# Fused waits, a later release of held stores, and two chunks taken whole, in a row-normalisation kernel on one core

One Trainium2 (trn2) chip, one core. The metric is the device time of the kernel in microseconds (us), of the slowest core, which here is the only one. "Span" is the profiled execution from first to last instruction; it is some 1.3 us shorter than the time.

## The reference

```python
# x: 16 x 1024 x 512 float32, gamma: 512 ones, eps: 1e-5
rms = np.sqrt(np.mean(x ** 2, axis=-1, keepdims=True) + eps)
return np.maximum(x / rms * gamma, 0)
```

That is 33.55 MB in and 33.55 MB out, and a few operations per element.

## The kernel before

The 16,384 rows are cut into 8 chunks; a chunk gives each of the 128 partitions 16 rows (32 KB), 4.19 MB in all. The kernel keeps room for six chunks ("slots") in SBUF. SyncE issues all loads and stores into one DMA queue. GpSimd passes "loaded" on to ScalarE, which squares and sums 8 rows at a time (a group) and takes the root. VectorE takes the reciprocal, scales 8 rows by 8 instructions, clamps the group at zero by a ninth (the relu), and reports `done`. Two waits hold stores back (groups, chunks and stores are counted from 0): stores 0 and 1 until the third row of group 5 (`tick3`), store 2 and all later ones until the first row of group 10 (`tick1`). Loads 6 and 7 reuse the slots of stores 0 and 1.

```python
def take(engine, sem, n):              # one separate semaphore instruction
    engine.wait_ge(sem, n)
    engine.sem_inc(sem, -n)
...
nc.sync.wait_ge(tick3, 6)
store(0)
store(1)
for s in range(2):
    nc.sync.wait_ge(sem_slot[s], 32)
    load(7 + s)                        # loads of chunks 6 and 7
nc.sync.wait_ge(tick1, 11)
for i in range(2, nchunks):
    store(i)                           # each waits for its chunk's two groups
...
with nc.vector.Fori(0, ngroups) as gi: # 16 groups
    take(nc.vector, sq, 1)
    ...
    nc.vector.reciprocal(out=rstd[...], in_=rms[...]).then_inc(sv, 1)
    take(nc.vector, sv, 1)
    for j in range(G):                 # 8 rows of 512
        r = nc.vector.scalar_tensor_tensor(out=row, in0=row, scalar=rstd[...],
                in1=gamma_sb, op0=ALU.mult, op1=ALU.mult)
        ...                            # j == 0: tick1, j == 2: tick3, j == 7: sv
    take(nc.vector, sv, 1)
    nc.vector.tensor_scalar_max(out=blk, in0=blk, scalar1=0.0).then_inc(done, 1)
```

Of the kernel before, what the change touches and what calls it, by code (L numbers as in the profile page):

```python
# [1 line left out]

# [4 lines left out]

F32 = mybir.dt.float32
ALU = mybir.AluOpType
ACTF = mybir.ActivationFunctionType  # L10


@with_exitstack
def kernel(
    ctx: ExitStack,
    tc: tile.TileContext,
    x: bass.AP,
    gamma: bass.AP,
    eps: bass.AP,
    out: bass.AP,  # L20
):




    nc = tc.nc
    P = nc.NUM_PARTITIONS

    x2 = x.flatten_outer_dims()
    out2 = out.flatten_outer_dims()  # L30
    n, d = x2.shape
    rows = n // P
    inv_d = 1.0 / d
    K = 16
    G = 8
    nchunks = rows // K
    nslots = 6
    ngroups = rows // G
    per = K // G
    xv = x2.rearrange("(c p k) d -> c p k d", p=P, k=K)  # L40
    ov = out2.rearrange("(c p k) d -> c p k d", p=P, k=K)

    def sbuf(name, shape):
        return nc.alloc_sbuf_tensor(name, shape, F32).ap()

    gseed = sbuf("gseed", [P, d])
    gamma_sb = sbuf("gamma_sb", [P, d])
    eps_sb = sbuf("eps_sb", [P, 1])
    ss = sbuf("ss", [P, rows])
    rms = sbuf("rms", [P, rows])  # L50
    rstd = sbuf("rstd", [P, rows])
    slots = sbuf("slots", [P, nslots * K * d])
    junk = nc.alloc_psum_tensor("junk", [P, G, d], F32).ap()


    loads = [(0, 0, G), (0, G, K - G)] + [(i, 0, K) for i in range(1, nchunks)]


    sem_half = nc.alloc_semaphore("half")
    sem_slot = [nc.alloc_semaphore(f"slot{s}") for s in range(nslots)]  # L60
    sem_g = nc.alloc_semaphore("gam")
    sem_z = nc.alloc_semaphore("zero")
    ready = nc.alloc_semaphore("ready")
    sq = nc.alloc_semaphore("sq")
    tick1 = nc.alloc_semaphore("tick1")
    tick3 = nc.alloc_semaphore("tick3")
    done = nc.alloc_semaphore("done")
    sa = nc.alloc_semaphore("sa")
    sv = nc.alloc_semaphore("sv")

    def slot_ap(i):
        s = (i % nslots) * K * d
        return slots[:, s:s + K * d].rearrange("p (k d) -> p k d", d=d)

    def load(m):
        i, a, r = loads[m]
        return nc.sync.dma_start(out=slot_ap(i)[:, a:a + r, :],
                                 in_=xv[i][:, a:a + r, :]
                                 ).then_inc(sem_half if m == 0 else sem_slot[i % nslots], 16)

    def take(engine, sem, n):
        engine.wait_ge(sem, n)
        engine.sem_inc(sem, -n)  # L83

    def store(i):
        nc.sync.wait_ge(done, per * (i + 1))
        nc.sync.dma_start(out=ov[i], in_=slot_ap(i)).then_inc(sem_slot[i % nslots], 16)



    ctx.enter_context(tc.manual_schedule(engines={mybir.EngineType.SP}))
    early = 2
    for m in range(early):
        t = load(m)
        tc.no_tile_sem_insts.add(t.ins.name)
    ctx.close()
    tc.close()
    tc.compile()  # L98

    for m, (i, a, r) in enumerate(loads):  # L100
        if m >= early and i < nslots:
            load(m)


    nc.sync.wait_ge(tick3, 6)
    store(0)
    store(1)
    for s in range(2):
        nc.sync.wait_ge(sem_slot[s], 32)
        load(7 + s)  # L110
    nc.sync.wait_ge(tick1, 11)
    for i in range(2, nchunks):
        store(i)

    for m, (i, a, r) in enumerate(loads):
        if m == 0:
            take(nc.gpsimd, sem_half, 16)
        else:
            nc.gpsimd.wait_ge(sem_slot[i % nslots], 32 * (i // nslots) + 16)
        nc.gpsimd.sem_inc(ready, r // G)  # L120

    nc.vector.memset(gseed, 0.0).then_inc(sem_z, 1)  # L122
    nc.vector.memset(eps_sb, eps).then_inc(sem_z, 1)  # L123

    nc.scalar.wait_ge(sem_z, 1)
    nc.scalar.dma_start(out=gseed[0:P:32, :],
                        in_=gamma[None, :].to_broadcast([P // 32, d])
                        ).then_inc(sem_g, 16)
    nc.scalar.preload_act_table(ACTF.Sqrt)  # L129
    take(nc.scalar, sem_z, 2)  # L130
    with nc.scalar.Fori(0, ngroups) as gi:
        take(nc.scalar, ready, 1)
        base = nc.scalar.snap((gi % (nslots * per)) * (G * d))
        col = nc.scalar.snap(gi * G)
        for j in range(G):
            a = nc.scalar.activation(  # L136
                out=junk[:, j, :], in_=slots[:, bass.ds(base + j * d, d)],
                func=ACTF.Square, accum_out=ss[:, bass.ds(col + j, 1)])
            if j == G - 1:
                a.then_inc(sa, 1)  # L140
        take(nc.scalar, sa, 1)
        nc.scalar.activation(out=rms[:, bass.ds(col, G)], in_=ss[:, bass.ds(col, G)],  # L142
                             func=ACTF.Sqrt, bias=eps_sb, scale=inv_d).then_inc(sq, 1)

    take(nc.vector, sem_g, 16)
    nc.vector.stream_shuffle(gamma_sb, gseed, [0] * 32)  # L146
    with nc.vector.Fori(0, ngroups) as gi:
        take(nc.vector, sq, 1)
        base = nc.vector.snap((gi % (nslots * per)) * (G * d))
        col = nc.vector.snap(gi * G)  # L150
        blk = slots[:, bass.ds(base, G * d)]
        nc.vector.reciprocal(out=rstd[:, bass.ds(col, G)],  # L152
                             in_=rms[:, bass.ds(col, G)]).then_inc(sv, 1)
        take(nc.vector, sv, 1)
        for j in range(G):
            row = slots[:, bass.ds(base + j * d, d)]
            r = nc.vector.scalar_tensor_tensor(  # L157
                out=row, in0=row, scalar=rstd[:, bass.ds(col + j, 1)], in1=gamma_sb,
                op0=ALU.mult, op1=ALU.mult)
            if j == 0:  # L160
                r.then_inc(tick1, 1)
            if j == 2:
                r.then_inc(tick3, 1)
            if j == G - 1:
                r.then_inc(sv, 1)
        take(nc.vector, sv, 1)
        nc.vector.tensor_scalar_max(out=blk, in0=blk, scalar1=0.0).then_inc(done, 1)  # L167

    take(nc.sync, done, ngroups)
    take(nc.sync, tick1, ngroups)  # L170
    take(nc.sync, tick3, ngroups)
    for i in range(nchunks - nslots, nchunks):
        take(nc.sync, sem_slot[i % nslots], 32 * (i // nslots + 1))


# [1 line left out]
_INS = ['x', 'gamma', 'eps']  # L177
_OUTS = [((16, 1024, 512), 'float32')]

_NUMBERS = {'eps': 9.999999747378752e-06}  # L180


# [26 lines left out]
```

## Time and profile before

| | before |
|---|---|
| time, median of 4 runs (lowest to highest) | 160.50 us (160.39 to 160.58) |
| span | 159.3 us |
| VectorE busy, share | 126.0 us, 79% |
| ScalarE busy, share | 86.3 us, 54% |
| share of the 16 DMA engines taken by the queue of loads and stores | 98.2% |
| mean rate of loads and stores together | 421 GB/s |

The share of the DMA engines is 98.2%, while VectorE, the busiest engine, has a fifth of the span idle. Beside the profile's pages I use two records that the trace holds: each DMA packet (start, length, size; 2,176 of them are data) and each instruction, the sequencers' own among them. "First packet" below is the first data packet of a load or a store; the queue "runs dry" when it has nothing left to move. To know how busy an engine was I lay the packets end to end on 16 engines, as the trace does not name the engine.

### The profile page before, as it was taken

The page shows a single profiled execution, that of the slowest core. Times are in us where ns is not written, and L with a number is a line of the kernel's source. Part 1 is how long each engine was busy: PE and PEld are TensorE (multiplying, and loading weights), DVE is VectorE, ACT ScalarE, POOL GpSimd, SP SyncE. Part 2 cuts the span into 40 slices and gives each one's busy share as a digit, 9 for nine tenths or more (in the row PEclk, how much of TensorE's full clock was granted, in tenths as well). Part 3 has the DMA queues.
Part 4 walks back from the last instruction along what each step waited for, and adds up shares of the span by engine and source line. Part 5 has one row for each costly group of instructions (what it writes and reads, how often), then busy time and mean ns, then how long its engine had stood idle before and what let it go on. Part 6 is the DMA issues. An engine that isn't in the chain of part 4 may idle for free. (4 is left out here: it accounts for less than half of the span.)

```text
span 159.3 us, 999 instructions
## 1 busy us (share of the span) xinstructions
DVE 126.0 (79%) x164; ACT 86.3 (54%) x273; POOL 0.2 (0%) x4
## 2 busy tenths in 40 slices
DVE  1012989898999999999999999999999989897000
ACT  0388929889989988988920098898500000000000
POOL 0000000000000000000000000000000000000000
DMA  6999999999999999999999999999999999999995
GB/s 193 405 453 424 502 395 395 502 420 395 453 469 395 395 502 420 395 428 494 395 395 444 461 411 395 486 436 395 453 453 403 411 494 411 403 461 453 395 420 247
DMA packets 2456, 67.12 MB, mean 421 GB/s; under 512 B 276, under 2 KB 276, under 8 KB 280
## 3 DMA queue, kind: packets, MB, share of 16 engines
q1 hardware_dynamic: 2448, 67.11, 98.2%
q10 hardware_dynamic: 8, 0.01, 0.0%
HBM read 33.56 MB, written 33.55 MB: 421 GB/s over the span
## 5 line engine op out<-in xcount | busy, mean ns | idle before, releaser
L157 DVE SCALAR_TENSOR_TENSOR slots<-slots,rstd,gamma_sb 128x512 f32 x128 | 86.2, 747 | 4.8 <-DVEq L83 4.8
L136 ACT ACTIVATE junk<-slots 128x512 f32 x128 | 74.4, 581 | 20.6 <-ACTq L83 20.3
L167 DVE TENSOR_SCALAR slots<-slots x16 | 36.7, 2294 | 2.4 <-DVEq L83 0.2
L136 ACT ACTIVATION_READ_ACCUMULATOR junk<-slots x128 | 23.9, 187 | 0.0
L152 DVE RECIPROCAL rstd<-rms x16 | 3.1, 197 | 5.3 <-DVEq L83 5.3
L142 ACT ACTIVATE rms<-ss,eps_sb x16 | 4.8, 301 | 3.0 <-ACTq L83 3.0
L146 DVE LOAD_MASK_SELECT gamma_sb<-gseed x1 | 0.0, 14 | 5.4 <-DVEq L83 5.4
L129 ACT ACT_TABLE_LOAD x1 | 1.3, 1283 | 4.2 <-issue 4.2
L122 DVE MEMSET gseed<- 128x512 f32 x1 | 0.5, 485 | 2.6 <-PEq L98 2.6
L146 DVE STREAM_SHUFFLE gamma_sb<-gseed 128x512 f32<-128x512 f32 x1 | 0.7, 723 | 0.0
L190 POOL MEMSET const-bfloat16-1.0<- 128x1 bf16 x1 | 0.1, 102 | 0.0
L190 POOL MEMSET const-uint8-127<- 128x1 uint8 x1 | 0.1, 102 | 0.0
L190 POOL MEMSET const-float32-0.0<- 128x1 f32 x1 | 0.1, 99 | 0.2 <-issue 0.2
L190 POOL MEMSET const-float32-1.0<- 128x1 f32 x1 | 0.1, 99 | 0.0
L123 DVE MEMSET eps_sb<- 128x1 f32 x1 | 0.1, 59 | 0.0
## 6 DMA issues: line engine op xcount, KB each, us to landing
out_dram<-slots SPq DMA_DIRECT2D x8, 4096.0 KB, 20.6
slots<-in_x_dram SPq DMA_DIRECT2D x7, 4096.0 KB, 29.7
slots<-in_x_dram SPq DMA_DIRECT2D x2, 2048.0 KB, 9.7
gseed<-in_gamma_dram ACTq DMA_DIRECT2D x1, 8.0 KB
```

The costliest lines, as they stand in the source:

```text
L122: nc.vector.memset(gseed, 0.0).then_inc(sem_z, 1)
L123: nc.vector.memset(eps_sb, eps).then_inc(sem_z, 1)
L129: nc.scalar.preload_act_table(ACTF.Sqrt)
L136: a = nc.scalar.activation(out=junk[:, j, :], in_=slots[:, bass.ds(base + j * d, d)], func=ACTF.Square, accum_out=ss[:, bass.ds(col + j, 1)])
L142: nc.scalar.activation(out=rms[:, bass.ds(col, G)], in_=ss[:, bass.ds(col, G)], func=ACTF.Sqrt, bias=eps_sb, scale=inv_d).then_inc(sq, 1)
L146: nc.vector.stream_shuffle(gamma_sb, gseed, [0] * 32)
L152: nc.vector.reciprocal(out=rstd[:, bass.ds(col, G)], in_=rms[:, bass.ds(col, G)]).then_inc(sv, 1)
L157: r = nc.vector.scalar_tensor_tensor(out=row, in0=row, scalar=rstd[:, bass.ds(col + j, 1)], in1=gamma_sb, op0=ALU.mult, op1=ALU.mult)
L167: nc.vector.tensor_scalar_max(out=blk, in0=blk, scalar1=0.0).then_inc(done, 1)
L190: nc = _bacc.Bacc("TRN2", target_bir_lowering=False, num_devices=1)
```

## The change

Its intent is to spend less of VectorE's time on waiting and on starting instructions. Waits no longer go by a separate instruction, but stand in front of the instruction that is to carry them, with the decrements moved to the end of the group. One tick at the sixth row (`G - 3`) replaces the two at the third and the first. The last two chunks are taken whole, by a reciprocal, a multiplication and a custom multiply-and-clamp. Two memsets move from VectorE to GpSimd. As the loop now ends before a slot is used again, its slot index no longer needs a remainder (`gi % 12` becomes `gi`). Cut to its core:

```diff
-    nc.sync.wait_ge(tick3, 6)
+    nc.sync.wait_ge(tick, 6)
...
-    nc.sync.wait_ge(tick1, 11)
+    nc.sync.wait_ge(tick, 11)
...
-    with nc.vector.Fori(0, ngroups) as gi:
-        take(nc.vector, sq, 1)
+    with nc.vector.Fori(0, ndyn) as gi:          # ndyn = 12
+        nc.vector.wait_ge(sq, 1)
         nc.vector.reciprocal(...).then_inc(sv, 1)
-        take(nc.vector, sv, 1)
+        nc.vector.wait_ge(sv, 1)
         for j in range(G):
             ...
-            if j == 0:
-                r.then_inc(tick1, 1)
-            if j == 2:
-                r.then_inc(tick3, 1)
-            if j == G - 1:
-                r.then_inc(sv, 1)
-        take(nc.vector, sv, 1)
+            if j == G - 3:
+                r.then_inc(tick, 1)
+        r.then_inc(sv, 1)
+        nc.vector.wait_ge(sv, 2)
         nc.vector.tensor_scalar_max(out=blk, in0=blk, scalar1=0.0).then_inc(done, 1)
+        nc.vector.sem_inc(sv, -2)
+        nc.vector.sem_inc(sq, -1)
+    for i in range(nslots, nchunks):             # chunks 6 and 7
+        nc.vector.wait_ge(sq, per * (i - nslots + 1))
+        nc.vector.reciprocal(out=fac, in_=rms[:, i * K:(i + 1) * K]).then_inc(sv, 1)
+        nc.vector.wait_ge(sv, steps + 1)
+        nc.vector.tensor_tensor(out=blk, in0=blk, in1=fac[...to P, K, d], op=ALU.mult).then_inc(sv, 1)
+        nc.vector.wait_ge(sv, steps + 2)
+        nc.vector._custom_dve(dve_ops.TENSOR_MUL_SAT, out=blk, in0=blk,
+            in1=gamma_sb[...to P, K, d], s0=float("inf"), s1=0.0).then_inc(done, per)
```

(ScalarE's loop gets the same treatment of its waits.)

More of the change, by code (lines that the diff above doesn't have):

```diff
@@ L4 @@
 import concourse.tile as tile
-from concourse import bass_utils, mybir
+from concourse import bass_utils, dve_ops, mybir
 from concourse._compat import with_exitstack
@@ L64 @@
     sq = nc.alloc_semaphore("sq")
-    tick1 = nc.alloc_semaphore("tick1")
-    tick3 = nc.alloc_semaphore("tick3")
+    tick = nc.alloc_semaphore("tick")
     done = nc.alloc_semaphore("done")
@@ L110 @@
         load(7 + s)
-    nc.sync.wait_ge(tick1, 11)
+    nc.sync.wait_ge(tick, 11)
     for i in range(2, nchunks):
         store(i)
+    nc.gpsimd.memset(gseed, 0.0).then_inc(sem_z, 1)
+    nc.gpsimd.memset(eps_sb, eps).then_inc(sem_z, 1)
     for m, (i, a, r) in enumerate(loads):
@@ L120 @@
         nc.gpsimd.sem_inc(ready, r // G)
-    nc.vector.memset(gseed, 0.0).then_inc(sem_z, 1)
-    nc.vector.memset(eps_sb, eps).then_inc(sem_z, 1)
     nc.scalar.wait_ge(sem_z, 1)
@@ L131 @@
     with nc.scalar.Fori(0, ngroups) as gi:
-        take(nc.scalar, ready, 1)
         base = nc.scalar.snap((gi % (nslots * per)) * (G * d))
         col = nc.scalar.snap(gi * G)
+        nc.scalar.wait_ge(ready, 1)
         for j in range(G):
@@ L138 @@
                 func=ACTF.Square, accum_out=ss[:, bass.ds(col + j, 1)])
-            if j == G - 1:
-                a.then_inc(sa, 1)
-        take(nc.scalar, sa, 1)
+        a.then_inc(sa, 1)
+        nc.scalar.wait_ge(sa, 1)
         nc.scalar.activation(out=rms[:, bass.ds(col, G)], in_=ss[:, bass.ds(col, G)],
                              func=ACTF.Sqrt, bias=eps_sb, scale=inv_d).then_inc(sq, 1)
-    take(nc.vector, sem_g, 16)
+        nc.scalar.sem_inc(sa, -1)
+        nc.scalar.sem_inc(ready, -1)
+    nc.vector.wait_ge(sem_g, 16)
     nc.vector.stream_shuffle(gamma_sb, gseed, [0] * 32)
-    with nc.vector.Fori(0, ngroups) as gi:
-        take(nc.vector, sq, 1)
-        base = nc.vector.snap((gi % (nslots * per)) * (G * d))
+    ndyn = nslots * per
+    with nc.vector.Fori(0, ndyn) as gi:
+        base = nc.vector.snap(gi * (G * d))
         col = nc.vector.snap(gi * G)
         blk = slots[:, bass.ds(base, G * d)]
+        nc.vector.wait_ge(sq, 1)
         nc.vector.reciprocal(out=rstd[:, bass.ds(col, G)],
                              in_=rms[:, bass.ds(col, G)]).then_inc(sv, 1)
-        take(nc.vector, sv, 1)
+        nc.vector.wait_ge(sv, 1)
         for j in range(G):
@@ L159 @@
                 op0=ALU.mult, op1=ALU.mult)
-            if j == 0:
-                r.then_inc(tick1, 1)
-            if j == 2:
-                r.then_inc(tick3, 1)
-            if j == G - 1:
-                r.then_inc(sv, 1)
-        take(nc.vector, sv, 1)
-        nc.vector.tensor_scalar_max(out=blk, in0=blk, scalar1=0.0).then_inc(done, 1)
+            if j == G - 3:
+                r.then_inc(tick, 1)
+        r.then_inc(sv, 1)
+        nc.vector.wait_ge(sv, 2)
+        nc.vector.tensor_scalar_max(out=blk, in0=blk, scalar1=0.0).then_inc(done, 1)
+        nc.vector.sem_inc(sv, -2)
+        nc.vector.sem_inc(sq, -1)
+    steps = 0
+    for i in range(nslots, nchunks):
+        blk = slot_ap(i)
+        fac = rstd[:, i * K:(i + 1) * K]
+        nc.vector.wait_ge(sq, per * (i - nslots + 1))
+        nc.vector.reciprocal(out=fac, in_=rms[:, i * K:(i + 1) * K]).then_inc(sv, 1)
+        nc.vector.wait_ge(sv, steps + 1)
+        nc.vector.tensor_tensor(out=blk, in0=blk, in1=fac[:, :, None].to_broadcast([P, K, d]),
+                                op=ALU.mult).then_inc(sv, 1)
+        nc.vector.wait_ge(sv, steps + 2)
+        nc.vector._custom_dve(
+            dve_ops.TENSOR_MUL_SAT, out=blk, in0=blk,
+            in1=gamma_sb[:, None, :].to_broadcast([P, K, d]),
+            s0=float("inf"), s1=0.0).then_inc(done, per)
+        steps += 2
     take(nc.sync, done, ngroups)
-    take(nc.sync, tick1, ngroups)
-    take(nc.sync, tick3, ngroups)
+    take(nc.sync, tick, ndyn)
+    take(nc.sync, sq, ngroups - ndyn)
+    take(nc.sync, sv, steps)
+    take(nc.sync, sem_g, 16)
     for i in range(nchunks - nslots, nchunks):
```

## The prediction

> **What bounds the kernel now.** I read the page first, parts 1 to 3, then the DMA packets one by one, then the queue that issues the transfers, then VectorE's waits and its timeline. Part 1 and part 3 together:
>
> ```profile
> span 159.3 us, 999 instructions
> DVE 126.0 (79%) x164; ACT 86.3 (54%) x273; POOL 0.2 (0%) x4
> ...
> DMA  6999999999999999999999999999999999999995
> ...
> q1 hardware_dynamic: 2448, 67.11, 98.2%
> ...
> HBM read 33.56 MB, written 33.55 MB: 421 GB/s over the span
> ```
>
> The reader is to see that VectorE (DVE) has a fifth of the span idle, while the one queue of loads and stores fills the 16 DMA engines for 98.2% of it. The packets say it more sharply: between the first data packet, at 1.75 us, and about 157.7 us, the engines' idle time is under 0.02 us in every stretch of 5 us. A chunk of 4.19 MB passes in 9.7 us, and 16 such passes (8 loads, 8 stores) are 155.2 us. With 1.75 us before them and 1 to 2 us for the last packets and their completion, that is the span. So the bound is the bytes. A change of VectorE cannot lower the time; it can only raise it, by letting the DMA queue run dry. There are three places where this can happen, the three where a store waits for VectorE and no other transfer is queued behind which it could hide. SyncE's timeline shows when they are issued:
>
> ```profile
> 0.73 4.16 SPq L77 DMA_DIRECT2D slots<-in_x_dram  x7
> 58.30 0.82 SPq L87 DMA_DIRECT2D out_dram<-slots  x2
> 71.23 10.35 SPq L77 DMA_DIRECT2D slots<-in_x_dram  x2
> 98.19 48.62 SPq L87 DMA_DIRECT2D out_dram<-slots  x6
> ```
>
> Columns: start, length, engine, line, operation. Store 0 goes out at 58.30 us, store 2 at 98.19, and the last one, store 7, at 146.475 (the end of the 48.62 us less its own 0.33). Their first packets started at 60.68, 99.58 and 147.99 us, each exactly when the packets before them ran out. From issue to first packet an idle queue needs some 1.02 us (first load: 0.73 to 1.75). So the spare time is 60.68 - 58.30 - 1.02 = **1.35 us** at store 0, 99.58 - 98.19 - 1.02 = **0.37 us** at store 2 and **0.5 us** at store 7. Those three figures are what the change can eat. The chain that ended last is of no help here (it ends in the last VectorE instruction and holds 1.5% of the span), because it does not follow DMA packets.
>
> VectorE's own pace, from the groups and the timeline of one group:
>
> ```profile
> L157 DVE SCALAR_TENSOR_TENSOR slots<-slots,rstd,gamma_sb 128x512 f32 x128 | 86.2, 747 | 4.8 <-DVEq L83 4.8
> L167 DVE TENSOR_SCALAR slots<-slots x16 | 36.7, 2294 | 2.4 <-DVEq L83 0.2
> ...
> L152 DVE RECIPROCAL rstd<-rms x16 | 3.1, 197 | 5.3 <-DVEq L83 5.3
> ```
>
> ```profile
> 55.70 0.20 DVE L152 RECIPROCAL rstd<-rms  x1
> 56.20 5.39 DVE L157 SCALAR_TENSOR_TENSOR slots<-slots,rstd,gamma_sb 128x512 f32 x8 [0.30 <-DVEq L83]
> 61.74 2.29 DVE L167 TENSOR_SCALAR slots<-slots  x1
> ```
>
> A group of 8 rows takes 8.24 us from reciprocal to reciprocal; the rows start every 0.6625 us. Per group 0.30 us pass between reciprocal and first row and 0.15 us between last row and relu. Both gaps are a separate semaphore instruction (line 83)[...].
>
> [...]
>
> **The change part by part.**
> (a) Waits carried by instructions. A DMA that carried its wait started 0.03 us after the releasing row (98.159 to 98.187). Add the 0.05 us from dispatch to start: a gap of about 0.08 us. Saving: 0.30 - 0.08 = 0.22 at the reciprocal and 0.15 - 0.08 = 0.07 at the relu, so **0.29 us a group**, period 7.95. The two decrements at the group's end lie beneath the relu's 2.29 us, as the loop's register work does now. ScalarE saves similar gaps in the first group (0.19 at the square root, 0.26 to the first reciprocal, some at its start): I take 0.4 us, the first reciprocal at 14.1 instead of 14.48.
> (b) The ticks. Store 0 waited for the third row of group 5, store 2 for the first row of group 10; now both for the sixth. That is 3 x 0.6625 = 2.0 us and 5 x 0.6625 = 3.3 us later in the group. Against it stand 0.4 + 0.22 + 5 x 0.29 = 2.07 us and 0.4 + 0.22 + 10 x 0.29 = 3.52 us. So store 0 goes out at 58.3 + 2.0 - 2.07 = 58.2 and store 2 at 98.2 + 3.3 - 3.5 = 98.0. Both stay in time, by 1.4 and 0.6 us. That the two later rows cancel the same saving per group twice is what a tuned choice would look like.
> (c) The last two chunks whole. One reciprocal 0.20,[...] and two gaps of 0.08: 17.86, less 0.09 of overlap: 17.8 us, where two groups take 16.5. It is slower by 1.3 us a chunk[...].
> (d) VectorE's end: 14.1 + 12 x 7.95 = 109.5, + 17.8 = 127.3 (store 6; now 130.0), + 17.8 = 145.1 (store 7; now 146.4). Store 7 then has 1.8 us to spare instead of 0.5. VectorE's busy time rises to 96 x 0.747 + 12 x 2.294 + 14 x 0.2[...] + 0.7 = 137.7 us.
> (e) The two memsets on GpSimd, beside a first load that lands at 8.3 us: gamma was ready at 9.2, five us before its first use. Nothing. SyncE's extra final takes pass while the last store is moving. Nothing.
> Sum: VectorE shorter by 1.3 us at its end, off the path; the DMA queue neither gains nor loses. The time stays at **160.5 us**.
>
> **The rivals.**
> Rival 1: the waits aren't carried by the row ops, since a register operation stands between wait and row; then the ticks come later than they pay for. With no saving at all store 0's first packet comes at 56.20 + 3.31 + 0.75 + 0.03 + 1.02 = 61.31, 0.6 us late; store 2's at 97.41 + 5.11 = 102.52, another 2.3 us late: 163.4 us, 1.8% slower. With half the saving only store 2 is late, by about 1.1: 161.6 us. For it: every row is preceded by such a register operation. Against it: SyncE's stores and ScalarE's gamma load carry their waits already.
> Rival 2: one of the whole-chunk instructions runs[...] (an operand broadcast with step 0, or a custom operation which no trace here shows).[...] Against it:[...] a wait for a slow op twice in a tuned kernel would be odd.
> Rival 3: a gain, because VectorE is nearly the bound at the end (0.5 us to spare). The packets speak against it: no idle time at 148 us is there to be removed.
>
> **Range and chances.** The main case (some 3 in 4) is 160.5 with run to run scatter of 0.1 to 0.2. Rival 1 in part or whole (about 1 in 5) makes 161 to 163.4, rival 2 (about 1 in 30) alone passes 2%. So the range is 160.1 to 161.8. Faster by over 2% would need fewer bytes: 0.01. Slower by over 2%: 0.04.
>
> **What would show it.** Right: DMA still near 98%, packets without idle time, gaps of about 0.08 us at reciprocal and relu, a period of 7.95 us in the first 12 groups, stores 0 and 2 issued near 58.2 and 98.0,[...] VectorE ending near 145 us. Wrong: a dip of the DMA row near 60 or 100 us with the stores issued after 59.7 or 98.6 (rival 1), or a whole-chunk instruction over 9 us and a dip near 148 us (rival 2); a time under 160 would mean that the first packet started earlier or that chunks passed in under 9.7 us, which nothing here foresees.

In (c) the length of each whole-chunk instruction is cut; with it the sum came to 17.86 us, and 17.8 after the overlap, while the terms left come to 0.36. In (d) VectorE's busy time came to 137.7 us, with four such instructions in it; the terms left come to 102.7. That length was my estimate and not read from a trace, and VectorE's ends of 127.3 and 145.1 us and the 1.8 us to spare at store 7 rest on it. That the transfers themselves could not be made faster is not shown by any run, as all use the same ones; what the trace shows is a chunk's 4.194 MB in 9.7 us, which is 432 GB/s. What stands between two instructions at a separate wait can be read in the kernel before: the reciprocal ends at 55.90 us, the semaphore instruction runs from 55.94 to 55.96, a register operation from 56.04 to 56.15 (0.115 us), and the row starts at 56.20, 0.05 us later.

## The result

The kernel after takes **160.32 us** (median of 4 runs, 160.23 to 160.65) against 160.50. The ratio is 0.9993, with a 95% interval of 0.9976 to 1.001: the same. All runs are fast ones, with a granted clock of 1.0. (A ratio here is the mean time of one kernel's fast runs over that of the other's fast runs of the same rounds, so not quite the ratio of the medians.)

The kernel after, parts 1 to 3 of its page:

```profile
span 159.0 us, 896 instructions
DVE 129.4 (81%) x128; ACT 86.3 (54%) x273; POOL 0.8 (0%) x6
...
DMA  6999999999999999999999999999999999999996
...
q1 hardware_dynamic: 2448, 67.11, 98.4%
```

VectorE is busier by 3 us, and the DMA row is as full as it was. SyncE's timeline of the kernel after (start, length, engine, line, operation):

```profile
0.73 4.06 SPq L77 DMA_DIRECT2D slots<-in_x_dram  x7
58.44 0.82 SPq L87 DMA_DIRECT2D out_dram<-slots  x2
71.21 10.46 SPq L77 DMA_DIRECT2D slots<-in_x_dram  x2
98.34 47.40 SPq L87 DMA_DIRECT2D out_dram<-slots  x6
```

Stores 0 and 2 go out within 0.15 us of where they went before, although their ticks sit 3 and 5 rows later in the group. Their first packets start at 60.71 and 99.52 us (before: 60.68 and 99.58), and store 7, issued at 145.41 instead of 146.48, has its first packet at 147.96 (147.99). Between 3 and 157 us at least 13 of the 16 engines (before) and 14 (after) move data at every moment; the odd ones are between two packets. VectorE in the kernel after, its costliest groups:

```profile
L158 DVE SCALAR_TENSOR_TENSOR slots<-slots,rstd,gamma_sb 128x512 f32 x96 | 64.7, 747 | 1.8 <-DVE rstd L153 1.8
L165 DVE TENSOR_SCALAR slots<-slots x12 | 27.5, 2294 | 0.4
...
L178 DVE CUSTOM_DVE_ANT_1 slots<-slots,gamma_sb 128x8192 f32<-128x8192 f32 x2 | 17.4, 8692 | 0.3
L175 DVE TENSOR_TENSOR slots<-slots,rstd 128x8192 f32<-128x8192 f32 x2 | 17.4, 8691 | 0.1
```

And its timeline, one group of the loop and the last chunk:

```profile
54.00 0.19 DVE L153 RECIPROCAL rstd<-rms  x1
54.35 5.39 DVE L158 SCALAR_TENSOR_TENSOR slots<-slots,rstd,gamma_sb 128x512 f32 x8 [0.15 <-DVE rstd L153]
59.77 2.29 DVE L165 TENSOR_SCALAR slots<-slots  x1
61.98 0.19 DVE L153 RECIPROCAL rstd<-rms  x1
...
127.59 0.25 DVE L173 RECIPROCAL rstd<-rms 128x16 f32<-128x16 f32 x1
127.87 8.69 DVE L175 TENSOR_TENSOR slots<-slots,rstd 128x8192 f32<-128x8192 f32 x1
136.69 8.69 DVE L178 CUSTOM_DVE_ANT_1 slots<-slots,gamma_sb 128x8192 f32<-128x8192 f32 x1
```

A group of the loop now takes 61.98 - 54.00 = 7.98 us (8.24 before). Before the first row 0.15 us are idle instead of 0.30; between the last row (54.35 + 5.39 = 59.74) and the clamp 0.03 us are left of 0.15. The last chunk takes 145.38 - 127.59 = 17.8 us, where its two groups took 16.5. So VectorE ends at 145.38 us instead of 146.44. None of this shortens the time, as the DMA engines had no idle time to give up (98.4% of the span is taken).

### The profile page after: what moved, and what is told of

It reads as the page before. It is cut to its first block, busy times and chain, and to the rows that moved or that the text cites. A ratio compares the mean times of both kernels' runs of the same rounds, so it can differ in the third digit from the quotient of the medians.

```text
span 159.0 us, 896 instructions
## 1 busy us (share of the span) xinstructions
DVE 129.4 (81%) x128; ACT 86.3 (54%) x273; POOL 0.8 (0%) x6
## 3 DMA queue, kind: packets, MB, share of 16 engines
q1 hardware_dynamic: 2448, 67.11, 98.4%
## 4 chain that ended last, share of the span: by engine, by line
DVE 51%; issue 19%; DMA 13%; DVEq 5%; ACT 3%; ACTq 0%; POOLq 0%
DVE slots L158 27%; DMA slots<-in_x_dram 13%; DVE slots L175 11%; DVE slots L178 11%; DVEq L158 3%; ACT junk L135 3%; DVE rstd L153 1%; DVEq L148 1%; DVEq L153 0%; ACTq L135 0%; DVE rstd L173 0%; DVE slots L165 0%; ACT rms L140 0%; DVEq L167 0%; DVEq L177 0%
## 5 line engine op out<-in xcount | busy, mean ns | idle before, releaser
L158 DVE SCALAR_TENSOR_TENSOR slots<-slots,rstd,gamma_sb 128x512 f32 x96 | 64.7, 747 | 1.8 <-DVE rstd L153 1.8
L165 DVE TENSOR_SCALAR slots<-slots x12 | 27.5, 2294 | 0.4
L178 DVE CUSTOM_DVE_ANT_1 slots<-slots,gamma_sb 128x8192 f32<-128x8192 f32 x2 | 17.4, 8692 | 0.3
L175 DVE TENSOR_TENSOR slots<-slots,rstd 128x8192 f32<-128x8192 f32 x2 | 17.4, 8691 | 0.1
L153 DVE RECIPROCAL rstd<-rms x12 | 2.3, 195 | 4.2 <-ACT rms L140 4.2
L115 POOL MEMSET gseed<- 128x512 f32 x1 | 0.5, 525 | 1.9 <-POOLq L98 1.9
L173 DVE RECIPROCAL rstd<-rms 128x16 f32<-128x16 f32 x2 | 0.5, 245 | 0.0
```

The source lines that it names most:

```text
L115: nc.gpsimd.memset(gseed, 0.0).then_inc(sem_z, 1)
L153: nc.vector.reciprocal(out=rstd[:, bass.ds(col, G)], in_=rms[:, bass.ds(col, G)]).then_inc(sv, 1)
L173: nc.vector.reciprocal(out=fac, in_=rms[:, i * K:(i + 1) * K]).then_inc(sv, 1)
L175: nc.vector.tensor_tensor(out=blk, in0=blk, in1=fac[:, :, None].to_broadcast([P, K, d]), op=ALU.mult).then_inc(sv, 1)
L178: nc.vector._custom_dve(dve_ops.TENSOR_MUL_SAT, out=blk, in0=blk, in1=gamma_sb[:, None, :].to_broadcast([P, K, d]), s0=float("inf"), s1=0. ...
```

## The experiments

The custom operation was not open to experiments, so the runs on the kernel after use `f_stt_last` as their base: the same kernel with a stock instruction in its place. All runs gave correct results. "Moved" is against `f_stt_last` where that is the base (medians; 160.31 us, on a chip where the kernel before took 160.65) and else against the kernel before. The runs were made in three calls, that is, batches on one chip each: `f`, `b` and `c`; `d`, `e` and `g`; `h`, `i` and `j`. The calls ran the kernel before at medians of 160.65, 160.72 and 160.60 us, so a difference of 0.1 us between calls means nothing.

What the packets show, for all runs (us; issue -> first packet of the store; the last column is when the first and the last of the 16 engines ended their data):

```
run               store 0         store 2          store 7          engines end
before            58.31 -> 60.68   98.19 ->  99.58  146.48 -> 147.99  157.66 to 158.74
after             58.44 -> 60.71   98.34 ->  99.52  145.41 -> 147.96  157.66 to 158.44
f_stt_last        58.57 -> 60.71   98.47 ->  99.56  145.49 -> 148.02  157.73 to 158.68
b_old_waits_row6  60.16 -> 61.00  101.37 -> 102.21  146.34 -> 150.90  160.62 to 160.80
c_row7            59.46 -> 60.70   99.36 -> 100.23  145.72 -> 148.91  158.59 to 160.09
c_gate_at_relu    62.20 -> 63.05  102.10 -> 102.94  145.47 -> 151.65  161.37 to 161.60
d_no_hold         30.26 -> 61.31   82.32 -> 100.11  145.44 -> 148.51  158.19 to 158.99
e_last_1us_late   58.52 -> 60.70   98.42 ->  99.55  146.42 -> 148.02  157.70 to 158.49
e_last_4us_late   58.46 -> 60.78   98.36 ->  99.62  149.55 -> 150.38  160.13 to 160.28
g_fused_16        58.82 -> 60.70   98.97 ->  99.81  142.77 -> 148.51  158.24 to 158.81
h_store0_row7     59.11 -> 60.64   98.35 ->  99.60  145.37 -> 148.00  157.68 to 158.55
i_store2_row7     58.74 -> 60.67   99.30 -> 100.14  145.66 -> 148.84  158.55 to 158.72
j_hold_store0     58.41 -> 60.62   81.70 ->  99.76  145.33 -> 148.17  157.84 to 158.72
```

### Is the custom operation special? (f_stt_last)

```diff
-        nc.vector._custom_dve(dve_ops.TENSOR_MUL_SAT, out=blk, in0=blk, in1=gamma..., s0=inf, s1=0.0)
+        nc.vector.scalar_tensor_tensor(out=blk, in0=blk, scalar=0.0, in1=gamma...,
+                                       op0=ALU.max, op1=ALU.mult)
```

> The custom multiply-and-clamp of the last two chunks (not open to experiments) is replaced by one scalar_tensor_tensor of 8,192 elements, relu first and then times gamma (the same result here, as gamma is all ones). Theory ([...]DMA queue never dry): each lasts 8.7 us as the custom one did (8.69), VectorE ends near 145.4 us, DMA share 98%, time 160.3 to 160.6. Rival (the custom operation is faster or slower than a stock one): another duration, VectorE's end moved by twice the difference, the time unchanged unless the end passes 146.9.

Measured: 160.31 us (160.23 to 160.53), ratio to before 0.9978 (0.9964 to 0.9991). Its last chunk in the timeline:

```profile
127.69 0.24 DVE L173 RECIPROCAL rstd<-rms 128x16 f32<-128x16 f32 x1
127.96 8.69 DVE L175 TENSOR_TENSOR slots<-slots,rstd 128x8192 f32<-128x8192 f32 x1
136.76 8.69 DVE L178 SCALAR_TENSOR_TENSOR slots<-slots,gamma_sb 128x8192 f32<-128x8192 f32 x1
```

The stock instruction lasts 8.69 us too. Rival 2 of the prediction falls: all three kinds of two-tensor instruction take the same 8.69 us for 8,192 elements, with an operand repeated by step 0 as well, so none of them is slower than the others. Nor is any slower than the row op: 8.69 us are 0.54 us for each 512 elements, where a row took 0.747.

### Would the later tick alone have cost time? (b_old_waits_row6)

```diff
 (on the kernel before)
-            if j == 0:
+            if j == G - 3:
                 r.then_inc(tick1, 1)
-            if j == 2:
-                r.then_inc(tick3, 1)
...
-    nc.sync.wait_ge(tick3, 6)
+    nc.sync.wait_ge(tick1, 6)
```

> The kernel before with its separate waits, but both held stores released by the sixth row: the change's tick without the change's savings. Theory (rival 1 of the prediction; 1.02 us from issue to first packet, and the queue dry for what is late): store 0 issued at 60.3, first packet 61.3, 0.6 us late; store 2 issued at 101.5, first packet 102.5, a further 2.3 late; time 163.4 us. Rival (what is queued inside the DMA engines hides a late issue): time 160.5, no idle engine near 61 and 100 us.

Measured: 162.60 us (162.54 to 162.75), ratio 1.0121 (1.0105 to 1.0136): 2 us lost, where 2.9 were expected. Store 2 goes out at 101.37 us. The sums by stretch show the dry queue; columns: stretch, its length, VectorE, ScalarE and GpSimd busy, TensorE's clock, DMA share, GB/s. First this run, then the kernel after:

```profile
98.00:100.00 2.00, 2.00 (x5) 2.00 (x7) 0.00 (x0) 1.00 1.21 524
100.00:102.00 2.00, 2.00 (x5) 2.00 (x7) 0.00 (x0) 1.00 0.00 0
102.00:104.00 2.00, 1.85 (x3) 1.52 (x6) 0.00 (x0) 1.00 1.25 524
```

```profile
98.00:100.00 2.00, 1.97 (x4) 2.00 (x9) 0.00 (x0) 1.00 1.18 508
100.00:102.00 2.00, 2.00 (x2) 1.89 (x8) 0.00 (x0) 1.00 0.69 295
102.00:104.00 2.00, 1.85 (x4) 1.63 (x6) 0.00 (x0) 1.00 1.18 508
```

(A packet's bytes seem to be counted at one moment, so a single stretch swings, from 0.69 to 1.18 in the second fence; but in no stretch of 2 us between 2 and 156 us does the share fall below 0.61 in the kernel before or after, and here it is 0.00 with 0 GB/s.) So the later tick costs 2 us unless the group's shorter period brings it forward. The rival, that a late issue is hidden, falls. From issue to first packet it was 0.84 us at both stores, not the 1.02 that I had taken from the first load.

### One row later, and one clamp later (c_row7, c_gate_at_relu)

```diff
 c_row7:          -            if j == G - 3:
                  +            if j == G - 2:
 c_gate_at_relu:  -    nc.sync.wait_ge(tick, 6)      +    nc.sync.wait_ge(done, 6)
                  -    nc.sync.wait_ge(tick, 11)     +    nc.sync.wait_ge(done, 11)
```

> The kernel after (with the stock op of f_stt_last), its tick moved from the sixth to the seventh row, 0.66 us later. Theory: store 0 issued at 59.1, first packet within time; store 2 issued at 99.0, first packet 100.0 instead of 99.5, so 0.5 us lost and 160.9 us. Rival (issue needs less than 1.02 us in a busy queue, or what is late is made up): 160.4 us, no idle time near 99.5 us.

Measured: 161.56 us (161.19 to 161.79), ratio to before 1.0044 (1.0031 to 1.0058), moved by +1.25 us against `f_stt_last`, where 0.5 was expected. The direction is the theory's, the size is not.

> The kernel after (stock op as in f_stt_last), its held stores released by the relu's end of groups 5 and 10 instead of the sixth row. Theory: store 0 issued at 62.1, first packet 63.1, 2.4 us late; store 2 issued at 102.0, first packet 103.0, 1.1 us more; time 163.8 us. Rival (late issue is hidden): 160.4 us.

Measured: 163.24 us (163.15 to 163.30), ratio 1.0156 (1.014 to 1.0172), moved by +2.9 us. The first packet of store 0 was 2.34 us late (63.05 against 60.71), as expected, that of store 2 3.38 us late; the time moved by 0.5 us less than that.

Two things are not in the theory. First, the time ends with the **last** engine. In `f_stt_last` 15 engines end by 158.03 us and one at 158.68. Where the queue ran dry, all 16 started together again (16 packets of 32 KB, 524 GB/s, in the microsecond from 150 us of `e_last_4us_late`, below), and ended together: within 0.23 us in `c_gate_at_relu`, 0.18 in `b_old_waits_row6`. That takes up part of the lost time, as the first packet tells of the foremost engine and the time of the hindmost. Second, a packet of 32 KB took 1.213 us in the median, but near 78 to 83 us, where the queue goes from store 1 to load 6, there are packets of up to 2.4 us in `b_old_waits_row6` and in these two runs. Above 1.213 us they cost, per engine, 0.94 us in `b_old_waits_row6`, some 0.7 in `c_row7`, 0.82 in `c_gate_at_relu`, 0.14 in the kernel before, and 0.04 in `f_stt_last` and in the kernel after. In `c_row7` the idle time near 100 us was only about 0.1 us per engine, so this slow handover, with an engine that ends at 160.09, makes up most of its loss.

### How late may the last store be? (e_last_1us_late, e_last_4us_late)

```diff
+        if i == nchunks - 1:
+            nc.vector.memset(junk[:, 0:2, :], 0.0)      # 0:8 for 4us
         nc.vector.scalar_tensor_tensor(out=blk, ...)
```

> The kernel after (stock op as in f_stt_last) with a memset of 1,024 elements of a scratch tile before the last multiply of the last chunk[...]. Theory: store 7 may be late by 147.96 - 145.41 - 1.02 = 1.5 us for nothing: time 160.4 us, store 7 issued near 146.6, first packet still at 148.0. Rival (VectorE is the bound at the end[...]): 161.5 us.

Measured: 160.35 us (160.25 to 160.52), ratio to before 0.9978 (0.9965 to 0.9991). The memset took 0.91 us. VectorE ended 0.94 us later (146.39 us), store 7 went out at 146.42, and its first packet started at 148.02, as without the delay. The theory holds; the rival, that VectorE is the bound at the end, falls.

> The same with a memset of 4,096 elements[...]. Theory: 1.5 us of it are hidden, 2.8 to 2.9 come through: store 7 issued near 149.8, first packet near 150.8, time 163.2 us. Rival (no slack): 164.8. Rival (all hidden): 160.4.

Measured: 162.11 us (162.00 to 162.15), ratio 1.0086 (1.0071 to 1.01), moved by +1.8 us. The memset took 3.47 us, after a gap of 0.93. VectorE ended 4.07 us later, at 149.53, and the queue ran dry; the run's stretches, then those of the kernel after:

```profile
148.00:149.00 1.00, 1.00 (x1) 0.00 (x0) 0.00 (x0) 1.00 0.01 0
149.00:150.00 1.00, 0.53 (x1) 0.00 (x0) 0.00 (x0) 1.00 0.00 0
150.00:151.00 1.00, 0.00 (x0) 0.00 (x0) 0.00 (x0) 1.00 1.22 524
```

```profile
148.00:149.00 1.00, 0.00 (x0) 0.00 (x0) 0.00 (x0) 1.00 1.15 492
149.00:150.00 1.00, 0.00 (x0) 0.00 (x0) 0.00 (x0) 1.00 1.21 524
150.00:151.00 1.00, 0.00 (x0) 0.00 (x0) 0.00 (x0) 1.00 1.14 492
```

No line of the second fence has an empty second. Store 7's first packet was 2.36 us late (150.38 against 148.02), 0.83 us after the issue. The time rose by 0.6 us less than that, and the engines ended within 0.15 us: the lagging engine had caught up while the others stood still. The expectation's own spare time, 1.5 us, taken from the measured 4.07 would have given 2.6; with the latency of 0.83 it is 2.4, and 1.8 after what the last engine takes up.

### Does an earlier end of VectorE pay? (g_fused_16_groups)

```diff
-    with nc.vector.Fori(0, ndyn) as gi:          # 12, then chunks 6 and 7 whole
+    with nc.vector.Fori(0, ngroups) as gi:       # 16, and nothing after it
```

> Only the fused waits and the row-six tick; all 16 groups in the loop, no whole chunks. Theory: period 7.98 us to the end, VectorE ends near 14.1 + 16 x 7.98 = 141.7 us, 3.7 us before the kernel after; the queue is full either way, so 160.4 us as well. Rival (the earlier end pays): up to 3 us less, or the straggling engine's last packet earlier than 158.4.

Measured: 160.58 us (160.55 to 160.66), ratio to before 0.999 (0.9977 to 1.0003). The last group in its timeline:

```profile
134.63 0.19 DVE L153 RECIPROCAL rstd<-rms  x1
135.03 5.39 DVE L158 SCALAR_TENSOR_TENSOR slots<-slots,rstd,gamma_sb 128x512 f32 x8 [0.20 <-DVE rstd L153]
140.45 2.29 DVE L165 TENSOR_SCALAR slots<-slots  x1
```

VectorE ended at 142.74 us, 2.6 us before the kernel after, and this bought nothing: taking two chunks whole makes VectorE later by 2.6 us in a place where it has that much to spare. My 141.7 was a us short. With all 16 groups in the loop the slot index needs its remainder again; the register operation before the first row then takes 0.115 us instead of 0.065, the gap 0.20 us instead of 0.15, and the period is 8.03 us. So this run is not only without whole chunks: store 2 left at 98.97 us, its first packet came 0.25 us later than in `f_stt_last`, and all runs were slower than those of `e_last_1us_late` (160.55 to 160.66 against 160.25 to 160.52). That the late store 2 makes this difference of 0.2 us is likely, but not shown. It does show that the fused waits alone save 8.24 - 8.03 = 0.21 us a group; the dropped remainder is worth the other 0.05.

### What is the hold for? (d_no_hold, j_hold_store0_only)

```diff
 d: -    nc.sync.wait_ge(tick, 6)
 d: -    nc.sync.wait_ge(tick, 11)
 j: -    nc.sync.wait_ge(tick, 11)
```

> The kernel after (stock op as in f_stt_last) without the hold: each store is issued as soon as its chunk is done, store 0 near 30 us and store 2 near 81.7 us. Theory (one queue served in order; the five chunks of loads issued at the start stay ahead): first packets of the stores at the same 60.7 and 99.5 us, time 160.4 us; the hold is then needed for nothing in this kernel. Rival (stores issued early mix with the loads and delay them, which is what the hold is for): chunks 1 to 5 land later than 22.7, 32.4, 42.1, 51.8, 61.5 us, VectorE or ScalarE waits for them, and the time rises by over 1 us.

Measured: 160.83 us (160.52 to 161.20), ratio to before 1.0007 (0.9995 to 1.0019). `e_last_1us_late`, which has the hold, took 160.35. So dropping both holds costs some 0.5 us. The loads were not delayed as a whole, so my rival falls in its mechanism (loads 1 to 5 start where they did), but the theory falls as well: packets of up to 2.0 us at 58 to 60 us, where the loads give way to store 0, cost 0.74 us per engine, and store 0's first packet comes 0.6 us later.

> The hold on store 0 kept (sixth row), that on store 2 dropped. d_no_hold lost 0.5 us, with packets of up to 2.0 us at 58 to 60 us (0.74 us per engine), where loads give way to a store that had been queued for 28 us, but 0.09 at 98 us. Theory: the first hold alone is worth it; here 160.3 to 160.4 us, packets at 58 us as in f_stt_last. Rival: both holds share the effect, 160.6 or more.

Measured: 160.36 us (160.28 to 160.53), ratio to before 0.9985 (0.9972 to 0.9998), the same as with both holds. There are no long packets at 58 us; some now stand at 98 us, where load 7 gives way to store 2 (0.33 us per engine). So the hold on store 0 is worth about half a us, and that on store 2 nothing that these runs can see.

### Which of the two late stores cost c_row7 its time? (h_store0_row7, i_store2_row7)

```diff
+            if j == G - 2:
+                r.then_inc(tick7, 1)
 h: -    nc.sync.wait_ge(tick, 6)     +    nc.sync.wait_ge(tick7, 6)
 i: -    nc.sync.wait_ge(tick, 11)    +    nc.sync.wait_ge(tick7, 11)
```

> As c_row7, but only store 0 waits for the seventh row; store 2 keeps the sixth. c_row7 lost 1.25 us against f_stt_last, of which the idle time near 100 us was only 0.1; 0.6 to 0.7 us per engine were in packets between 78 and 83 us that took up to 2.4 us instead of 1.21, where the queue goes from store 1 to load 6. Theory A (a store 0 issued less than some 1.5 us ahead of its turn makes that later handover slow): store 0 issued near 59.2, no idle time at 60.7, but slow packets at 78 to 82 us again, chunks 6 and 7 some 0.5 us later, time 160.8 to 161. Theory B (only the late store 2 costs): time 160.3, handover as in f_stt_last (0.05 us per engine).

Measured: 161.01 us, in six runs of 160.40, 162.13, 161.43, 160.32, 161.68 and 160.59; ratio to before 1.0038 (1.0006 to 1.007). The scatter is the result: three executions are as fast as ever, three lose 1 to 2 us. The profile fell on one of the fast ones (160.40, issue at 59.11), in which the handover at 78 to 82 us cost 0.16 us per engine, so it does not show the slow ones from inside. This is for theory A in its main point, and not a proof of its mechanism.

> As c_row7, but only store 2 waits for the seventh row. Issued near 99.1, first packet 0.84 us later (the latency of the late stores of the earlier runs) at 100.0 instead of 99.56. Theory A: 0.4 us late, some of it taken up by the lagging engine: time 160.4 to 160.8, no slow packets at 78 to 82 us. Theory B: all of c_row7's loss, 161.5 us.

Measured: 160.42 us (160.27 to 160.44), ratio to before 0.9985 (0.9972 to 0.9998). Its SyncE timeline:

```profile
58.74 0.83 SPq L88 DMA_DIRECT2D out_dram<-slots  x2
71.58 10.18 SPq L78 DMA_DIRECT2D slots<-in_x_dram  x2
99.30 46.69 SPq L88 DMA_DIRECT2D out_dram<-slots  x6
```

Store 2's first packet came at 100.14 us, 0.58 later than in `f_stt_last`, and the time moved by 0.1. All 16 engines ended between 158.55 and 158.72, so the lag of the last engine had hidden nearly all of the late start. Theory B falls: the half us late at store 2 is nearly free when it comes alone. What is left for c_row7's loss is its store 0, which was in time by the count of first packets. As only three of six executions of `h_store0_row7` lost time, and all five of `c_row7`, it stays untested whether the two late stores act together.

**What stays open**: why a store 0 issued at 59.1 us or later instead of 58.3 to 58.8 makes packets slow twenty us later, in some executions only, and why one queued for 28 us makes them slow at once. The runs show where it happens and what it costs, not what happens inside the DMA engines. That the difference between 160.31 and the before's 160.65 (ratio 0.9978) comes from the change, and not from one lagging engine's luck, is not shown either: the first measurement of the kernel after gave 0.9993. But three more runs with the change, `e_last_1us_late`, `i_store2_row7` and `j_hold_store0_only`, came out at 0.9978, 0.9985 and 0.9985, with intervals below 1, so a gain of about 0.2% may be real; no run here names its cause.

No version beat the kernel after by more than the scatter, so none is proposed.

## Why the prediction was right

**The bound.** Right, and shown. The queue of loads and stores has no idle time in either kernel, an earlier end of VectorE bought nothing (`g_fused_16_groups`), a later one within its spare time cost nothing (`e_last_1us_late`), and one beyond it did (`e_last_4us_late`). One reading of the prediction needs a word: the idle time was under 0.02 us per engine in every stretch of 5 us but one, as from 5 to 10 us I now count 0.023.

**The waits.** The sum was 0.29 us a group; measured 8.24 - 7.98 = 0.26. Both terms were off, in opposite directions. The wait for the reciprocal did not go onto the row itself but onto the register operation ahead of it (rival 1's reason, half true): that operation is recorded with the wait, 0.04 us after the reciprocal's end, then takes 0.065 us, and the row starts 0.05 us later. So 0.15 us are left instead of 0.08. That operation took 0.115 us before, and still does in `g_fused_16_groups`: carrying the wait brought the gap from 0.30 to 0.20 only, and the dropped remainder, which the prediction did not count, the rest. The clamp carries its wait itself and starts 0.03 us after the last row, where I had 0.08. That the errors nearly cancelled in the sum was luck. The first reciprocal came at 14.09 us, for 14.1 predicted.

**The ticks.** Predicted 58.2 and 98.0 us, measured 58.44 and 98.34; the 0.03 us a group (5 and 10 groups of it) and the 0.07 us by which the gap in the store's own group was longer than predicted explain the difference. The balance of a later row against earlier groups was the right step, and `b_old_waits_row6` shows what it was worth.

**The whole chunks.** Predicted 17.8 us for a chunk, measured 17.8; one instruction took 8.69 us. VectorE's end: 145.1 predicted, 145.38 measured.

**VectorE's busy time** was predicted at 137.7 us and is 129.4. The mis-sized term is above all "96 x 0.747" = 71.7: rows overlap by 0.084 us, and the page counts an overlap once (64.7 us for 96 rows), which is 7.0 of the 8.3 us. The page before would have told: 86.2 us for 128 rows is 0.673 a row, not 0.747. Nothing rested on it.

**The memsets.** The gamma row was ready at 9.9 us instead of 9.2, and its first use was at 14.4. No cost, as predicted.

**The spare time** is where the account was too simple, though the verdict did not depend on it. It took 1.02 us from issue to first packet and a loss of one us for each us beyond. The runs show 0.83 to 0.87 us for a late store; the last engine's lag takes up another half us or so of lateness (store 2 and store 7); and at store 0 the time suffers before the queue runs dry (`c_row7`, `h_store0_row7`). So "1.35 us to spare at store 0" was too much and "0.37 at store 2" too little. Rival 1's price, 163.4 us with no saving at all, came out at 162.6.

**Rivals 2 and 3** fell: 8.69 us for both whole-chunk instructions, and no gain clear of noise.

## What to carry to other kernels

Where the DMA queue has no idle time (98.2 and 98.4% of the engines' span here), ask of a change on a compute engine only one thing: does any transfer that waits for it get its issue before the queue runs out? When the pace of a loop changes, events tied to its iterations drift by the saving times the iteration number (here 0.26 us a group, 2.6 us at group 10), so a tick placed by hand has to be placed anew. An instruction saved off the path that sets the end buys spare time, which is worth having only if something else can spend it (here an end of VectorE 2.6 us earlier, in `g_fused_16_groups`, left the time at 160.58 us).

## What the runs measured beside the question

- A wait done by a separate instruction left 0.30 us idle before the first row and 0.15 before the clamp (the kernel before); carried by the next instruction, it left 0.20 (`g_fused_16_groups`, with the same slot index) and 0.03.
- A float32 tensor_tensor of 8,192 elements took 8,691 ns (the kernel after). A custom two-tensor operation (the kernel after) and a whole-chunk scalar_tensor_tensor (`f_stt_last`) of the same size took 8.69 us too. The row op, a scalar_tensor_tensor of 512 elements with a scalar for each partition, took 747 ns.
- Where the queue was dry, these runs show 0.83 to 0.87 us from the start of the issuing instruction to the first packet, which is about 0.5 us from that instruction's end (it lasts 0.33 to 0.35 us).
- Two effects decided the sub-microsecond part. One of the 16 engines ended 0.3 to 0.7 us after the rest in seven of the profiles, the kernels before and after among them, and within 0.03 us of it in the four in which a late store left the queue dry (`b_old_waits_row6`, `c_gate_at_relu`, `e_last_4us_late`, `i_store2_row7`). And packets where the queue goes from stores to loads or back took up to 2.4 us instead of 1.21 (`b_old_waits_row6`, `c_row7`, `c_gate_at_relu`).
